# A ConvGLU down projection in Strassen products, alternating with the gate and up products

## The chip, the cores and the metric

One Trainium2 chip, and one of its cores. The metric is the time of one execution on the device in microseconds. Three runs of the kernel before took 2771.68, 2771.95 and 2773.0 us; the median is 2771.95.

## The reference

One layer of a decoder trunk over 512 tokens of width 2048, all in float32: a mixer (a linear recurrence and an RWKV group side by side), then a feed-forward block with a convolution in its gate, then a gated embedding and a last norm. The change concerns the middle one:

```python
        h = h + jnp.concatenate([out_a, out_b], axis=-1) @ w_o[i]

        u = rmsnorm(h, ln_ffn[i])
        gate = causal_dwconv(u @ w_gate[i], conv_f_w[i], conv_f_b[i])
        h = h + (jax.nn.gelu(gate) * (u @ w_up[i])) @ w_down[i]

        u = rmsnorm(h, ln_ple[i])
        e = jax.nn.sigmoid(u @ w_ple_gate[i]) * (p[i] @ w_ple_proj[i])
        h = h + rmsnorm(e, ln_ple_post[i])
```

The hidden width D_FF is 6144, so `w_gate` and `w_up` are 2048 x 6144 and `w_down` is 6144 x 2048. The convolution has three taps and runs along the tokens.

## The kernel before

**Numbers.** To keep float32 accuracy, every operand of a large product is split in two: hi is the operand rounded to the matmul's short format, lo is what is left. A product is three matmuls into the same PSUM bank, whi·xh, whi·xl and wlo·xh (L148, L150, L152 in `dense`).

**The weight queue.** All weights come through one queue. `wfill_` (L103) takes the next item, has SP load it into one of two `wraw` buffers, lets ACT round it to `whi` (L118) and DVE subtract to `wlo` (L119). There are three buffers of each (HL), and the queue runs two items ahead (LOOK): a unit's hi and lo may be written as soon as the unit three before it has been read by PE. Each item is 512 KB, 128 partitions by 1024 numbers. `wnext` hands an item to the matmuls. The Tile scheduler orders each engine's instructions by dependences and priorities; the queue has a raised priority (offw). Nothing is written by hand in the FFN.

**The stages.** `phase1` is the mixer (0 to about 880 us). `phase2` starts with the second half of the output projection w_o, which ends at 955.5 us, and writes the residual `hT`: 16 tiles of 128 features by 512 tokens, features on the partitions. Each of its tiles is scaled by ln_ffn and split into `uh`, `ul` (the list u2). Then comes the FFN:

- `gate_up(f)` makes tile f of 48 of the hidden activation: two groups of 48 matmuls, in which weights stand and the 512 tokens of uh and ul move, 512 columns each. Then DVE scales the gate (L1120) and adds the two earlier taps (L1124), ACT does the first tap and the GELU, POOL multiplies by the norm's factor (L1126), DVE multiplies by up (L1130), and the tile is split: into `xh`, `xl` for chunks 0, 2 and 4, into `hh`, `hl` for chunks 1, 3 and 5. 
- `down(ch)` follows for each chunk of eight tiles (FC = 8, six chunks): 16 output tiles of 24 matmuls each, the chunk's tiles moving, weights standing, and an addition of each into hT on DVE (L1146).
- In the last chunk each finished tile of hT is also scaled and split (u3), squared on ACT and summed on POOL into `acc` (L1159), and transposed by PE, four 128 x 128 blocks (L1162), into `h3`, the residual with tokens on the partitions.

The work of `ffn_order` is plain: eight gate/up tiles, the first tile of the next chunk, then the down product of the finished chunk, and so on.

Behind the FFN, the embedding stage first needs the norm's factor: `tok_rstd` multiplies `acc` by ones on PE (L177) and takes the root on POOL. Then `gate` (L1198 to L1200) multiplies with tokens on the output partitions: blocks of u3 stand and the weights move, 512 columns each. The last stretch of this stage and the output follow; the change gives other buffers to some of its small tiles, since hh and hl are gone.

PSUM has six banks `mm` and two banks `wk`.

Of the kernel before, what the change touches and what calls it, by code (L numbers as in the profile page):

```python
# [21 lines left out]
FC = 8  # L22
# [57 lines left out]
class Builder:  # L80
# [22 lines left out]
    def wfill_(self):  # L103
        nc = self.nc
        while self.wn < len(self.wq) and len(self.wt) < self.LOOK:
            src, shape, *own = self.wq[self.wn]
            self.wn += 1
            if self.wraw:
                raw = self.wraw.pop(0)
            else:  # L110
                raw = self.t(self.cp, "wraw", shape, bufs=self.RAW)
                nc.sync.dma_start(raw, src)
            if own:
                hi, lo = (self.t(self.k2, n, shape, F32R, bufs=1) for n in own)
# [936 lines left out]

    def ffn_order(self):
        nch = NF // FC
        o = []
        for ch in range(nch):
            o += [("f", f) for f in range(ch * FC + (1 if ch else 0), (ch + 1) * FC)]
            if ch + 1 < nch:
                o.append(("f", (ch + 1) * FC))
            o.append(("d", ch))
        return o  # L1060

    def ffn_items(self):
# [3 lines left out]
        for o in self.ffn_order():  # L1066
            if o[0] == "f":
                r += [(A["wgu"][o[1], g, i], u) for g in range(2) for i in range(2)]
            else:
                r += [(A["wd"][o[1], m], u) for m in range(KT)]  # L1070
# [5 lines left out]
        r += [(A["wpg3"][1, 0, :, 2 * i:2 * i + 2], (128, 2, 256), "hl%d" % i, "hl%d" % (2 + i)) for i in range(2)]  # L1076
# [5 lines left out]
    def phase2(self):  # L1082
# [5 lines left out]
        hx = lambda i: (T("hh%d" % i, dt=F32R), T("hl%d" % i, dt=F32R))  # L1088
# [21 lines left out]
        hid = {}  # L1110

        def gate_up(f):
            pg = self.mm()
            self.run(self.dense(pg, 2, u2))
            if f == 0:
                r_ = self.tok_rstd(acc, D, RMS_EPS, k2)
                pu = self.mm()
                self.run(self.dense(pu, 2, u2))
                self.rstd_bcast(acc, D, RMS_EPS, k2, rs, r_)
            V.tensor_tensor(gz[:, 2:S + 2], pg, rs, ALU.mult)  # L1120
            c = T("tmp", 2)
            SC.activation(c, gz[:, 2:S + 2], AF.Identity, scale=self.P("cfw", 2 * NF + f), bias=self.P("cfb", f))
            for w in range(2):
                V.scalar_tensor_tensor(c, gz[:, w:w + S], self.P("cfw", w * NF + f), c, ALU.mult, ALU.add)  # L1124
            SC.activation(c, c, AF.Gelu_apprx_tanh)  # L1125
            G.tensor_tensor(c, c, rs, ALU.mult)  # L1126
            if f:
                pu = self.mm()
                self.run(self.dense(pu, 2, u2))
            V.tensor_tensor(c, c, pu, ALU.mult)  # L1130
            i = f % KT
            hi, lo = self.xsplit(i) if i < 8 else hx(i - 8)
            self.split(hi, lo, c)
            hid[f] = (hi, lo)

        self.acc3 = None
        u3 = []
        h3 = None

        def down(ch):  # L1140
            nonlocal h3
            last = ch == NF // FC - 1
            for m in range(KT):
                pd = self.mm()
                self.run(self.dense(pd, 1, [hid[ch * FC + i] for i in range(FC)]))
                V.tensor_tensor(hT[m], hT[m], pd, ALU.add)  # L1146
                if last:
                    hi, lo = T("uh%d" % m, dt=F32R), T("ul%d" % m, dt=F32R)
                    self.split(hi, lo, hT[m], self.P("ln_ple", m))
                    u3.append((hi, lo))  # L1150
                    if m == 0:
                        self.acc3 = T("acc")
                        SC.activation(self.acc3, hT[m], AF.Square)
                        h3 = [self.bp.tile([128, S], F32, tag="x%s%d" % ("hl"[i // 8], i % 8), name="h3_%d" % i, bufs=1)
                              for i in range(16)]
                    else:
                        sq = T("tmp", 2)
                        SC.activation(sq, hT[m], AF.Square)
                        G.tensor_tensor(self.acc3, self.acc3, sq, ALU.add)  # L1159
                    pt = self.aux()  # L1160
                    for tt in range(4):
                        TE.transpose(pt[:, tt * 128:(tt + 1) * 128], hT[m][:, tt * 128:(tt + 1) * 128], self.K("ident"))  # L1162
                    for tt in range(4):
                        SC.activation(h3[tt * 4 + m // 4][:, (m % 4) * 128:(m % 4 + 1) * 128],
                                      pt[:, tt * 128:(tt + 1) * 128], AF.Copy)

        for o in self.ffn_order():
            gate_up(o[1]) if o[0] == "f" else down(o[1])


        B = lambda i, nm_: T("h%s%d" % ("hl"[i // 8], i % 8))
        BR = lambda i, nm_: T("h%s%d" % ("hl"[i // 8], i % 8), dt=F32R)
        rsp = self.tok_rstd(self.acc3, D, RMS_EPS, k2)
        rsh = k2.tile([128, 4], F32, name="rsh")
# [180 lines left out]
```

## Time and profile before

| what | value |
|---|---|
| median of three runs | 2771.95 us |
| profiled execution | 2769.29 us |
| its span, from the first to the last instruction | 2767.5 us |
| mean granted clock of PE | 0.991 |
| PE busy | 98% of the span |
| FFN, first gate product to last down product | 955.5 to 2541.4 us |
| DMA over the span | 94 GB/s |

A row of instructions in the profile names the line, the engine, the operation and the tiles (output<-inputs), then partitions x elements. PE is the matmul engine, PEld its loading of the standing operand, DVE and ACT the vector and scalar engines, POOL the third elementwise engine, SP the queue that issues DMAs. A row of a wait names the engine and line that waits, and behind `<-` the one that released it. A matmul's busy time is modelled (it overlaps with the next one), so a price for one is taken here from starts, or from a stretch without gaps divided by its count.

### The profile page before, as it was taken

Reading aid. Unit: us, or ns where it says so; the run is one execution under the profiler, and the core shown is the slowest. Engines: PE = TensorE matmul, PEld = TensorE weight load, DVE = VectorE, ACT = ScalarE, POOL = GpSimd, SP = SyncE. Lnnn points to the kernel's source line nnn. Section 1 sums busy time; section 2 is a strip of 40 time slices with the busy share of each in tenths; the row PEclk is TensorE's granted clock in tenths of the full one; section 3 lists DMA queues with packets and bytes.
Section 4 is the critical chain, followed back from the end, with each engine's and each line's share of the span. In section 5 each row is a group of like instructions: output and inputs, shape, how many; then the busy total and the mean of one; then the engine's idle time right before and its main releaser. Section 6 shows DMA issues by size and latency. Waiting matters only on the chain.

```text
span 2767.5 us, 43105 instructions
## 1 busy us (share of the span) xinstructions
PE 2706.2 (98%) x18648; PEld 2216.3 (80%) x18648; DVE 1315.0 (48%) x1761; ACT 955.0 (35%) x1408; POOL 291.4 (11%) x232
## 2 busy tenths in 40 slices
PE   8999999999999999999999999999999999999996
PEld 7877777787787888888888888888888888887886
DVE  7784876668654433333333333333333333344235
ACT  6453455446433322212222222222122212234334
POOL 4010101101111300000000000000000000012013
PEclk9999999999999999999999999999999999999998
DMA  5221221222332322232222222222222222223322
GB/s 170 89 80 57 79 73 60 80 70 92 100 116 81 106 94 97 99 99 92 99 99 92 99 95 96 99 99 92 99 91 99 99 94 97 99 92 111 99 91 99
DMA packets 81886, 261.34 MB, mean 94 GB/s; under 512 B 9504, under 2 KB 12192, under 8 KB 81696
## 3 DMA queue, kind: packets, MB, share of 16 engines
q1 hardware_dynamic: 81696, 258.58, 28.3%
q8 instruction: 146, 2.39, 0.4%
q14 instruction: 44, 0.36, 0.0%
HBM read 250.42 MB, written 8.13 MB: 93 GB/s over the span
## 4 chain that ended last, share of the span: by engine, by line
PE 90%; DVE 5%; ACT 2%; POOL 1%; issue 1%; DMA 1%; SPq 0%; DVEq 0%; POOLq 0%
PE mm L152 25%; PE mm L148 25%; PE mm L150 25%; PE mm L1199 2%; PE mm L1198 2%; PE mm L1200 2%; PE wk L765 2%; PE wk L723 1%; DVE wlo L119 1%; PE wk L732 1%; DVE lrc L595 1%; PE ch L844 0%; PE ch L859 0%; PE wk L902 0%; DVE e L1231 0%
## 5 line engine op out<-in xcount | busy, mean ns | idle before, releaser
L118 ACT ACTIVATE whi<-wraw 128x1024 fp32r<-128x1024 f32 (+2 forms) x449 | 468.4, 1043 | 1368.5 <-PE mm L150 1244.7
L119 DVE TENSOR_TENSOR wlo<-wraw,whi 128x1024 fp32r<-128x1024 f32 (+2 forms) x449 | 554.7, 1235 | 487.0 <-ACT whi L118 482.1
L148 PE MATMUL mm<-uh,whi 128*128 128x512 f32 x1536 | 597.7, 389 | 0.0
L152 PE MATMUL mm<-uh,wlo 128*128 128x512 f32 x1536 | 597.5, 389 | 0.0
L150 PE MATMUL mm<-ul,whi 128*128 128x512 f32 x1536 | 597.5, 389 | 0.0
L148 PE MATMUL mm<-xh,whi 128*128 128x512 f32 x1216 | 481.8, 396 | 1.5 <-DVE y L885 0.9
L152 PE MATMUL mm<-xh,wlo 128*128 128x512 f32 x1216 | 481.3, 396 | 1.5 <-DVE wlo L119 1.5
L150 PE MATMUL mm<-xl,whi 128*128 128x512 f32 x1216 | 480.9, 395 | 0.0
L150 PEld LDWEIGHTS mm<-ul,whi 128*128 128x128 f32 x1536 | 288.3, 188 | 60.0
L152 PEld LDWEIGHTS mm<-uh,wlo 128*128 128x128 f32 x1536 | 288.3, 188 | 59.8
L148 PEld LDWEIGHTS mm<-uh,whi 128*128 128x128 f32 x1536 | 288.3, 188 | 59.8
L152 PEld LDWEIGHTS mm<-xh,wlo 128*128 128x128 f32 x1216 | 229.4, 189 | 52.1 <-issue 2.8
L148 PEld LDWEIGHTS mm<-xh,whi 128*128 128x128 f32 x1216 | 229.7, 189 | 51.6 <-issue 3.8
L150 PEld LDWEIGHTS mm<-xl,whi 128*128 128x128 f32 x1216 | 229.4, 189 | 48.5 <-issue 1.3
L1146 DVE TENSOR_TENSOR hT<-hT,mm 128x512 f32<-128x512 f32 x96 | 66.1, 688 | 320.1 <-PE mm L152 320.1
L1126 POOL TENSOR_TENSOR tmp<-tmp,rsa 128x512 f32<-128x512 f32 x48 | 62.4, 1300 | 1405.1 <-ACT tmp L1125 1405.1
L150 PE MATMUL mm<-hl,whi 128*128 128x512 f32 x384 | 152.9, 398 | 0.0
L148 PE MATMUL mm<-hh,whi 128*128 128x512 f32 x384 | 151.6, 395 | 0.0
L152 PE MATMUL mm<-hh,wlo 128*128 128x512 f32 x384 | 151.6, 395 | 0.0
L1130 DVE TENSOR_TENSOR tmp<-tmp,mm 128x512 f32<-128x512 f32 x48 | 33.0, 688 | 160.5 <-PE mm L152 158.4
L1199 PE MATMUL mm<-wlo,uh 128*128 128x512 f32 (+1 forms) x304 | 107.1, 352 | 0.0
L1200 PE MATMUL mm<-whi,ul 128*128 128x512 f32 (+1 forms) x304 | 107.0, 352 | 0.0
(435 smaller groups left out, 2855.1 us busy)
## 6 DMA issues: line engine op xcount, KB each, us to landing
wraw<-wgu SPq DMA_DIRECT2D x192, 512.0 KB, 3.2
wraw<-wd SPq DMA_DIRECT2D x96, 512.0 KB, 3.2
wraw<-wz SPq DMA_DIRECT2D x80, 512.0 KB, 3.5
wraw<-wpg SPq DMA_DIRECT2D x31, 512.0 KB, 3.3
wraw<-wo SPq DMA_DIRECT2D x24, 512.0 KB, 3.3
wraw<-wo SPq DMA_DIRECT2D x16, 256.0 KB, 2.7
tmp<-xT SPq DMA_DIRECT2D x16, 256.0 KB, 2.7
out<-e SPq DMA_DIRECT2D x16, 256.0 KB, 2.5
```

Of the source, the lines that this page charges most:

```text
L118: nc.scalar.activation(hi, raw, AF.Copy)
L119: nc.vector.tensor_tensor(lo, raw, hi.bitcast(F32), ALU.subtract)
L148: nc.tensor.matmul(ps, hi[:, k, :], xh, start=first and i == 0, stop=False)
L150: nc.tensor.matmul(ps, hi[:, k, :], xl, start=False, stop=False)
L152: nc.tensor.matmul(ps, lo[:, k, :], xh, start=False, stop=last and i == n - 1)
L765: TE.matmul(ps[r_, i * 16:(i + 1) * 16], lhs(r_, c_, i), rhs(r_, i), start=True, stop=True)
L1126: G.tensor_tensor(c, c, rs, ALU.mult)
L1130: V.tensor_tensor(c, c, pu, ALU.mult)
L1146: V.tensor_tensor(hT[m], hT[m], pd, ALU.add)
L1198: TE.matmul(pg[tt], u3[k + i][0][:, ts_], wh[:, i, :], start=k + i == 0, stop=False)
L1199: TE.matmul(pg[tt], u3[k + i][0][:, ts_], wl[:, i, :], start=False, stop=False)
L1200: TE.matmul(pg[tt], u3[k + i][1][:, ts_], wh[:, i, :], start=False, stop=k + i == KT - 1)
```

## The change

The down projection is done another way and at other times.

**Chunks of four tiles.** FC goes from 8 to 4: twelve chunks, 512 hidden features each.

**Seven products.** Of eleven chunks the product is cut into quarters: two halves of the tokens by two halves of the 512 hidden features, and two halves of the weights' rows by two halves of their columns. A Strassen scheme (Winograd's form) makes the four output quarters from seven products of quarters where eight would be plain. It is done for two column halves b, so a chunk has 14 products. `product` has the tokens on the output partitions: 128-token blocks of the activations stand, 512 columns of weights move, 12 matmuls in two PSUM banks for one product. `down` adds each bank to what it belongs to (the table ADDS): directly to h3, the residual with tokens on partitions, or to two running sums `qx` and `qz`, 36 additions a chunk on DVE (line 1267 of the changed kernel). After the last of these chunks 20 additions bring qx and qz into h3.

**Their operands.** `hidden` forms from the four tiles (kept in `raw`) the seven sums of quarters and splits each into hi and lo; the tiles `hid` lie where xh8 to xl15 lay. `down_unit` loads a column half's four weight quarters in turn into `hw0` to `hw3`, and forms the weight sums in place or in `hw4` on DVE (lines 1091, 1094, 1100, 1104); every product's weight then goes through the queue as an item of the same size as before, split on lines 121 and 122. The weight array `wd` is laid out anew on the host.

**The order.** `ffn_order` alternates: after the chunk's four tiles and the first of the next, a product, then a half of a gate or up tile (24 matmuls) of the next chunk, and so on; 12 such halves are spread over the 14 products. Gate and up of all tiles from the fifth on use the two `wk` banks.

**The last chunk** is done plainly (`down_last`), 512 columns by 512 columns: two units of 24 matmuls each, then four additions to h3.

**Transposes.** h3 is now needed from the start: `turn` transposes hT in 64 blocks during the first four tiles. And the embedding stage needs features on partitions: `to_features` transposes h3 back after each column block of the last chunk, 64 blocks, and splits them out of PSUM into u3 (hi on ACT, lo on DVE).

**The norm's factor.** `to_features` squares on ACT with a running sum per token (`ss3`), and DVE and POOL turn these into the factor beside the embedding stage's first products. POOL's sum `acc` and the step through PE are gone there.

The diff, cut to its core:

```diff
-FC = 8
+FC = 4
...
-            if self.wraw:
+            if callable(src):
+                raw = src()
+            elif self.wraw:
                 raw = self.wraw.pop(0)
...
     def ffn_order(self):
+        g = lambda f: [("g", f, w, h) for w in range(2) for h in range(2)]
+        o = sum([g(f) for f in range(FC)], [])
         nch = NF // FC
-        o = []
-        for ch in range(nch):
-            o += [("f", f) for f in range(ch * FC + (1 if ch else 0), (ch + 1) * FC)]
-            if ch + 1 < nch:
-                o.append(("f", (ch + 1) * FC))
-            o.append(("d", ch))
+        for ch in range(nch - 1):
+            q = [("q", ch, b, i) for b in range(2) for i in range(7)]
+            o += g((ch + 1) * FC)
+            n = sum([g((ch + 1) * FC + i) for i in range(1, FC)], [])
+            k = 0
+            for i, x in enumerate(q):
+                o.append(x)
+                e = (i + 1) * len(n) // len(q)
+                o += n[k:e]
+                k = e
+        o += [("d", cb, kh) for cb in range(4) for kh in range(2)]
         return o
+    def down_unit(self, ch, b, i):
...
+        if i == 0:
+            self.q = {(0, 0): load(0, 0), (0, 1): load(0, 1)}
+            return self.q[0, 0]
+        if i == 1:
+            self.q[1, 1] = load(1, 1)
+            self.qt = self.t(self.k2, "hw4", (128, 2, 512), bufs=1)
+            V.tensor_tensor(self.qt, self.q[0, 0], self.q[0, 1], ALU.add)
+            return self.qt
+        if i == 2:
+            V.tensor_tensor(self.qt, self.qt, self.q[1, 1], ALU.add)
+            return self.qt
+        if i == 3:
+            self.q[1, 0] = load(1, 0)
+            return self.q[1, 1]
+        if i == 4:
+            V.tensor_tensor(self.q[0, 1], self.q[0, 1], self.q[1, 1], ALU.add)
+            return self.q[0, 1]
+        if i == 5:
+            return self.q[1, 0]
+        V.tensor_tensor(self.qt, self.qt, self.q[1, 0], ALU.add)
+        return self.qt
...
-        hx = lambda i: (T("hh%d" % i, dt=F32R), T("hl%d" % i, dt=F32R))
...
+        def turn(cb):
+            for tt in range(4):
+                pt = self.mm()
+                for i in range(4):
+                    TE.transpose(pt[:, i * 128:(i + 1) * 128], hT[4 * cb + i][:, tt * 128:(tt + 1) * 128], self.K("ident"))
+                SC.activation(h3[tt * 4 + cb], pt, AF.Copy)
...
+            d = tile(F32)
+            o = [None] * 7
+            o[0] = pair(a(0, 0))
+            V.tensor_tensor(d, a(1, 0), a(1, 1), ALU.subtract)
+            o[1] = pair(d)
+            V.tensor_tensor(d, d, a(0, 0), ALU.subtract)
+            o[2] = pair(d)
+            V.tensor_tensor(d, d, a(0, 1), ALU.add)
+            o[3] = pair(d)
+            V.tensor_tensor(d, a(0, 0), a(1, 0), ALU.subtract)
+            o[4] = pair(d)
+            o[5] = pair(a(0, 1))
+            o[6] = pair(a(1, 1))
+            return o
...
+        ADDS = [[(QX, ALU.add), (st(0, 0), ALU.add)], [(QZ, ALU.add)], [(QX, ALU.add)], [(st(0, 1), ALU.add)],
+                [(st(1, 1), ALU.subtract), (st(1, 0), ALU.add)], [(st(0, 0), ALU.add)], [(st(1, 0), ALU.add)]]
+
+        def product(ps, x, w, tt, first, last):
+            ts_ = slice(tt * 128, (tt + 1) * 128)
+            for k in range(2):
+                TE.matmul(ps, x[0][:, k, ts_], w[0][:, k, :], start=first and k == 0, stop=False)
+                TE.matmul(ps, x[0][:, k, ts_], w[1][:, k, :], start=False, stop=False)
+                TE.matmul(ps, x[1][:, k, ts_], w[0][:, k, :], start=False, stop=last and k == 1)
+
+        def down(ch, b, i):
+            w = self.wnext()
+            ps = [self.mm(), self.mm()]
+            for tt in range(2):
+                product(ps[tt], self.hids[ch][i], w, tt, True, True)
+            for at, op in ADDS[i]:
+                for tt in range(2):
+                    o = at(tt, b)
...
+                        V.tensor_tensor(o, o, ps[tt], op)
+
+        def down_last(cb, kh):
+            if kh == 0:
+                self.pd = [self.mm() for tt in range(4)]
+            w = self.wnext()
+            for tt in range(4):
+                product(self.pd[tt], self.hids[NF // FC - 1][kh][tt // 2], w, tt % 2, kh == 0, kh == 1)
+            if kh == 1:
+                for tt in range(4):
+                    h = h3[tt * 4 + cb]
+                    V.tensor_tensor(h, h, self.pd[tt], ALU.add)
...
+        def to_features(cb):
+            for tt in range(4):
+                sq = T("tmp", 2)
+                SC.activation(sq, h3[tt * 4 + cb], AF.Square, accum_out=ss3[:, tt * 4 + cb:tt * 4 + cb + 1])
+            for m in range(4 * cb, 4 * cb + 4):
+                pt = self.aux()
+                for tt in range(4):
+                    TE.transpose(pt[:, tt * 128:(tt + 1) * 128], h3[tt * 4 + cb][:, (m % 4) * 128:(m % 4 + 1) * 128], self.K("ident"))
+                hi, lo = T("uh%d" % m, dt=F32R), T("ul%d" % m, dt=F32R)
+                self.split(hi, lo, pt, self.P("ln_ple", m))
+                u3[m] = (hi, lo)
...
-        rsp = self.tok_rstd(self.acc3, D, RMS_EPS, k2)
...
+                V.tensor_reduce(t_.unsqueeze(2), ss3.rearrange("p (t c) -> p t c", c=4), mybir.AxisListType.X, ALU.add)
...
-    o["wd"] = f(g["w_down"][0].reshape(NF // FC, FC, 128, KT, 128).transpose(0, 3, 2, 1, 4))
+    o["wd"] = f(g["w_down"][0].reshape(NF // FC, 2, 2, 128, 2, 2, 512).transpose(0, 5, 1, 4, 3, 2, 6))
```

Two places show how the instructions stand in the rows. The first is PE near the end of the down projection, in the kernel before: the last chunk's first tile of the residual (hT1 here) is transposed inside the matmuls of the next output tile (mm is a PSUM bank, wk the transposed tile, con the identity):

```order
L152 MATMUL mm_2694_19739<-hh0_2493_18174,wlo_2681_19632 128x512
L148 MATMUL mm_2694_19739<-hh1_2574_18820,whi_2680_19631 128x512
L1162 MATMUL wk_2693_19730<-con_59,hT1_8388 128x128 x4
L150 MATMUL mm_2694_19739<-hl1_2575_18821,whi_2680_19631 128x512
L152 MATMUL mm_2694_19739<-hh1_2574_18820,wlo_2681_19632 128x512
```

In the changed kernel, PE at the end of the first of the last chunk's four column blocks. The block's tiles h3_0, h3_4, h3_8 and h3_12 hold the four token blocks:

```order
L1254 MATMUL mm_3206_20871<-whi_3193_20823,hid_3202_20865 128x512
L1291 MATMUL wk_3217_20944<-con_59,h3_0_10621 128x128
L1291 MATMUL wk_3217_20944<-con_59,h3_4_10625 128x128
L1291 MATMUL wk_3217_20944<-con_59,h3_8_10629 128x128
L1291 MATMUL wk_3220_20953<-con_59,h3_0_10621 128x128
L1291 MATMUL wk_3220_20953<-con_59,h3_4_10625 128x128
L1291 MATMUL wk_3220_20953<-con_59,h3_8_10629 128x128
L1252 MATMUL mm_3229_20980<-whi_3208_20874,hid_3195_20852 128x512
L1291 MATMUL wk_3217_20944<-con_59,h3_12_10633 128x128
L1291 MATMUL wk_3220_20953<-con_59,h3_12_10633 128x128
```

The transposes have moved from the middle of the next tile's matmuls to right behind the unit whose sums they read; one matmul of the next block stands between them.

The second place is DVE. In the kernel before, in the down product of the first chunk, it has these rows (wlo is a weight's lo part, hT the residual):

```order
L119 TENSOR_TENSOR wlo_1742_12198<-wraw_1740_12195,whi_1741_12197 128x1024
L1146 TENSOR_TENSOR hT11_8398<-hT11_8398,mm_1739_12194 128x512
L119 TENSOR_TENSOR wlo_1746_12230<-wraw_1744_12227,whi_1745_12229 128x1024
L1146 TENSOR_TENSOR hT12_8399<-hT12_8399,mm_1743_12226 128x512
L119 TENSOR_TENSOR wlo_1750_12262<-wraw_1748_12259,whi_1749_12261 128x1024
```

In the changed kernel, DVE at the start of a column half of a later chunk, where two products follow each other (hw4 and hw2 hold weight sums and quarters, qx and h3 what the products are added to, row and tmp belong to the gate of the next chunk's tile):

```order
L1192 TENSOR_TENSOR row_1537_10619<-wk_2983_19523,rsa_87 128x512
L122 TENSOR_TENSOR wlo_3000_19620<-wraw_2998_19617,whi_2999_19619 128x1024
L1196 SCALAR_TENSOR_TENSOR tmp_2997_19611<-row_1537_10619,par_58,tmp_2997_19611 128x512
L1267 TENSOR_TENSOR qx_1538_10637<-qx_1538_10637,mm_3001_19623 128x512
L1196 SCALAR_TENSOR_TENSOR tmp_2997_19611<-row_1537_10619,par_58,tmp_2997_19611 128x512
L1267 TENSOR_TENSOR qx_1538_10637<-qx_1538_10637,mm_3002_19624 128x512
L122 TENSOR_TENSOR wlo_3004_19643<-hw4_2994_19580,whi_3003_19642 128x1024
L1267 TENSOR_TENSOR h3_1_10622<-h3_1_10622,mm_3001_19623 128x512
L1104 TENSOR_TENSOR hw4_2994_19580<-hw4_2994_19580,hw2_3011_19693 128x1024
L122 TENSOR_TENSOR wlo_3010_19666<-wraw_3008_19663,whi_3009_19665 128x1024
```

Where one addition stood between two splits, there now stand additions out of two banks, a weight sum and the gate's convolution.

More of the change, by code (lines that the diff above doesn't have):

```diff
@@ L113, in wfill_ @@
             if own:
-                hi, lo = (self.t(self.k2, n, shape, F32R, bufs=1) for n in own)
+                w = self.t(self.k2, own[0], (128, 2) + shape[1:], F32R, bufs=1)
+                hi, lo = w[:, 0], w[:, 1]
             else:
@@ L1108, in phase2 @@
         G.memset(gz[:, 0:2], 0.0)
[L1110 to L1155, printed above, removed]
-                    else:
[L1157 to L1165, printed above, removed]
@@ L1167, in phase2 @@
[L1167 to L1177 removed]
+        h3 = [self.bp.tile([128, S], F32, tag="x%s%d" % ("hl"[i // 8], i % 8), name="h3_%d" % i, bufs=1) for i in range(16)]
@@ new lines, in turn, with half @@
+        def turn(cb):
[4 more added lines that the diff above has]
+                SC.activation(h3[tt * 4 + cb], pt, AF.Copy)
+        def half(ps, us, h):
+            wh, wl = self.wnext()
+            for k in range(8):
+                xh, xl = us[8 * h + k]
+                TE.matmul(ps, wh[:, k, :], xh, start=h + k == 0, stop=False)
+                TE.matmul(ps, wh[:, k, :], xl, start=False, stop=False)
+                TE.matmul(ps, wl[:, k, :], xh, start=False, stop=h == 1 and k == 7)
@@ new lines, in phase2, with gate_up @@
+        raw = [None, None]
+        pgu = [None, None]
+        gc = None
+        def gate_up(f, which, h):
+            nonlocal gc
+            if h == 0:
+                pgu[which] = self.aux() if f >= FC else self.mm()
+            half(pgu[which], u2, h)
+            if h == 0:
+                return
+            if which == 0:
+                if f == 0:
+                    self.r2 = self.tok_rstd(acc, D, RMS_EPS, k2)
+                    return
+            elif f == 0:
+                self.rstd_bcast(acc, D, RMS_EPS, k2, rs, self.r2)
+            if which == 0 or f == 0:
+                V.tensor_tensor(gz[:, 2:S + 2], pgu[0], rs, ALU.mult)
+                gc = c = T("tmp", 2)
+                SC.activation(c, gz[:, 2:S + 2], AF.Identity, scale=self.P("cfw", 2 * NF + f), bias=self.P("cfb", f))
+                for w in range(2):
+                    V.scalar_tensor_tensor(c, gz[:, w:w + S], self.P("cfw", w * NF + f), c, ALU.mult, ALU.add)
+                SC.activation(c, c, AF.Gelu_apprx_tanh)
+                G.tensor_tensor(c, c, rs, ALU.mult)
+            if which == 1:
+                i = f % FC
+                if i % 2 == 0:
+                    raw[i // 2] = T("hw%d" % (5 + i // 2), 1, (128, 2, 512))
+                V.tensor_tensor(raw[i // 2][:, i % 2, :], gc, pgu[1], ALU.mult)
+                if i < 4:
+                    turn(i) if f < FC else None
+                if i == FC - 1:
+                    self.hids[f // FC] = hidden(f == NF - 1)
@@ new lines, in phase2, with hidden, tile, pair @@
+        a = lambda i, j: raw[j][:, :, 256 * i:256 * i + 256]
+        def hidden(last):
+            n = 0
+            def tile(dt):
+                nonlocal n
+                t = self.bp.tile([128, 2, 256], dt, tag="x%s%d" % ("hl"[n // 8], 8 + n % 8), name=self.nm("hid"), bufs=1)
+                n += 1
+                return t
+            def pair(src):
+                hi, lo = tile(F32R), tile(F32R)
+                self.split(hi, lo, src)
+                return hi, lo
+            if last:
+                return [[pair(a(i, j)) for i in range(2)] for j in range(2)]
+            d = tile(F32)
[12 more added lines that the diff above has]
+            return o
@@ new lines, in phase2 @@
+        for o in self.ffn_order():
+            if o[0] == "g":
+                gate_up(*o[1:])
+            elif o[0] == "q":
+                down(*o[1:])
+                if o[1:] == (NF // FC - 2, 1, 6):
+                    for b in range(2):
+                        for q, at, op in ((QX, st(1, 0), ALU.add), (QX, st(0, 1), ALU.subtract), (QZ, st(0, 1), ALU.add),
+                                          (QX, st(1, 1), ALU.subtract), (QZ, st(1, 1), ALU.add)):
+                            for tt in range(2):
+                                V.tensor_tensor(at(tt, b), at(tt, b), q(tt, b), op)
+            else:
+                down_last(*o[1:])
+                if o[2] == 1:
+                    to_features(o[1])
```

70 lines of the change are left out of this document (47 added, 23 removed).

## The prediction

> **What bounds the kernel now.** I read the page's engine shares first, then the list of what PE waits for, then the stretches of the FFN one by one.
>
> ```profile
> span 2767.5 us, 43105 instructions
> PE 2706.2 (98%) x18648; PEld 2216.3 (80%) x18648; DVE 1315.0 (48%) x1761; ACT 955.0 (35%) x1408; POOL 291.4 (11%) x232
> ...
> PE 90%; DVE 5%; ACT 2%; POOL 1%; issue 1%; DMA 1%; SPq 0%; DVEq 0%; POOLq 0%
> ```
>
> ```profile
> PE wk L177 <- POOL acc L1159: 1.1, 1, 1.1
> ```
>
> PE is busy for 98% of the span and carries 90% of the chain that ended last. The row below the page's is the whole list of PE's waits from 955 to 2600 us: one wait, at the step out of the FFN. Inside the FFN there is none, so it costs what its matmuls cost. The next view cuts it into stretches (from and to, length, then busy time of PE, PEld, DVE, ACT, POOL with instruction counts, granted clock, DMA share, GB/s). The first two rows are the start and the first eight gate/up tiles, the next five are down chunks 0 to 4, then chunk 5 with its transposes, then the step into the embedding stage. The last row is a piece of the output projection before the FFN.
>
> ```profile
> 955.53:979.05 23.52, 23.52 (x113) 19.71 (x112) 6.38 (x7) 6.18 (x7) 3.77 (x2) 1.00 0.26 90
> 979.05:1153.25 174.20, 174.20 (x771) 144.24 (x770) 68.40 (x75) 50.31 (x59) 11.70 (x9) 1.00 0.29 97
> 1153.25:1240.29 87.04, 87.04 (x385) 72.07 (x384) 31.22 (x33) 17.54 (x18) 0.00 (x0) 1.00 0.29 97
> 1414.37:1503.96 89.59, 89.59 (x385) 72.08 (x384) 31.27 (x33) 17.56 (x18) 0.00 (x0) 1.00 0.28 94
> 1678.06:1765.10 87.04, 87.04 (x386) 72.07 (x384) 31.21 (x33) 17.54 (x18) 0.00 (x0) 1.00 0.29 97
> 1939.18:2028.77 89.59, 89.59 (x386) 72.07 (x384) 31.25 (x33) 17.57 (x18) 0.00 (x0) 1.00 0.28 94
> 2202.86:2289.90 87.04, 87.04 (x385) 72.07 (x384) 31.21 (x33) 17.54 (x18) 0.00 (x0) 1.00 0.29 97
> 2442.22:2541.35 99.13, 99.13 (x454) 77.99 (x452) 45.01 (x51) 46.43 (x110) 24.03 (x14) 1.00 0.29 94
> 2541.35:2549.47 8.12, 6.99 (x29) 5.42 (x28) 1.92 (x4) 1.47 (x6) 2.78 (x2) 0.79 0.81 245
> 890.50:901.40 10.90, 10.90 (x50) 9.03 (x49) 10.10 (x13) 8.57 (x15) 5.32 (x4) 1.00 0.52 168
> ```
>
> A chunk has 384 matmuls, so one costs 87.04/384 = 0.2267 us, with no gap at all. Chunks 1 and 3 take 89.59 (0.2333 each); their moving tiles are hh and hl, where chunks 0, 2 and 4 stream xh and xl. DVE has 31 us of work in 87, so it is far from the limit today.
>
> **The change, part by part.**
>
> *Matmuls removed.* The first eleven chunks of four tiles now cost 14 products of 12 matmuls, 11 x 168 = 1,848, and the twelfth stays plain with 192: 2,040 instead of 2,304. Each still moves 512 columns, but weights move and activations stand. The gate stage of the embedding does that already:
>
> ```profile
> 2600.08 0.39 PE L1199 MATMUL mm<-wlo,uh 128*128 128x512 f32 x1
> ...
> 2603.94 0.39 PE L1198 MATMUL mm<-whi,uh 128*128 128x512 f32 x1
> ```
>
> The second starts 17 matmuls after the first: 3.86/17 = 0.227, the same price. The tiles hh and hl are gone; the products read whi, wlo and tiles in the old xh8 to xl15 slots. I take 0.2267 for all 2,040, 462.5 us; the upper bound is 0.2333, the price with hh and hl, which adds 13.6.
>
> What they replace: chunks 0 to 4, 3 x 87.04 + 2 x 89.59 = 440.3; chunk 5, 99.13 less four early embedding matmuls (0.9), 98.2, its transposes included. And the step into the embedding stage:
>
> ```profile
> 2542.59 0.40 PE L1251 MATMUL mm<-whi,hl 128*128 128x512 f32 x1
> 2544.11 1.05 PE L177 MATMUL wk<-con,acc 128*128 128x1 f32 x8 [1.13 <-POOL acc L1159]
> ...
> 2546.32 0.63 PE L1200 MATMUL mm<-whi,ul 128*128 128x512 f32 x1
> ...
> 2548.88 0.52 PE L1200 MATMUL mm<-whi,ul 128*128 128x512 f32 x1
> ```
>
> PE waits 1.13 us for POOL's running sum of squares, does eight one-column products, and then runs six matmuls in 2.56 us, 0.427 each, at a clock that the window row gives as 0.79 on average. In 8.12 us start 18 full matmuls, worth 4.1; the other 4.0 us are wait, small products and half clock. The change takes that sum with accumulating squares on ACT and DVE and has no PE step there, so the 4.0 go. Before: 440.3 + 98.2 + 4.0 = 542.5 us.
>
> *What a gap costs.* The Trainium skill's page "TensorE: Matmul & The Clock Gate" (Part 1, What's actually happening) says that the clock halves only after a whole idle window of about 3.4 us. The trace differs: here 1.13 us idle and a thin spell of small products were enough, and the slow matmuls behind them, some eight at 0.2 us extra, cost another 1.6 us. By the page a 1 us wait would cost 1 us, by the row up to 2.8, and my upper bounds use the row.
>
> *Transposes added.* Chunk 5 now has 64; the change has 64 early (turn, four batches of 16 after the first four tiles) and 64 late (to_features).
>
> ```profile
> 2448.76 0.66 PE L1162 MATMUL wk<-con,hT 128*128 128x128 f32 x4
> ...
> 2454.85 0.66 PE L1162 MATMUL wk<-con,hT 128*128 128x128 f32 x4
> ```
>
> Between these lie 24 matmuls of 0.2333 (5.60) in 6.09 us: 0.5 us for four. 32 such fours: 16 us. Bounds: by columns, a quarter of 0.2267 each, 7.3; by the rows' own busy time, 0.66 for four, 21.
>
> *Late waits.* After each late pair of down units PE transposes what DVE has just added (the first pair of order pieces in the section on the change). Before, one unit's matmuls stood between a transpose and its addition; now only six short transposes and one matmul do, and two wk tiles then have to be split before the next two. The cover is about 0.8 us against one addition of 0.688 (row below) and its semaphores. I take 1 us a block, 4 us; bounds 0 and 4 x 2.8 = 11.
>
> *DVE and ACT.* This is where the change could give its gain back. DVE rows of the FFN (by form; mean ns of one is the number before the second bar):
>
> ```profile
> L119 DVE TENSOR_TENSOR wlo<-wraw,whi 128x1024 fp32r<-128x1024 f32 x272 | 333.3, 1225 | 344.5 <-ACT whi L118 340.3 <-PE wk L190 4.2
> L1124 DVE SCALAR_TENSOR_TENSOR tmp<-row,par,tmp 128x512 f32<-128x512 f32 x96 | 71.9, 749 | 2.6 <-ACT tmp L1122 0.9
> L1146 DVE TENSOR_TENSOR hT<-hT,mm 128x512 f32<-128x512 f32 x80 | 55.1, 688 | 269.3 <-PE mm L152 269.3
> L1120 DVE TENSOR_TENSOR row<-mm,rsa 128x512 f32<-128x512 f32 x48 | 33.2, 692 | 154.2 <-PE mm L152 154.2
> L132 DVE TENSOR_TENSOR xl<-tmp,xh 128x512 fp32r<-128x512 f32 x24 | 16.5, 686 | 0.0
> ```
>
> ```profile
> L118 ACT ACTIVATE whi<-wraw 128x1024 fp32r<-128x1024 f32 x272 | 288.6, 1061 | 1006.0 <-PE mm L150 1001.4 <-PE mm L152 4.7
> ```
>
> A new chunk of four tiles has on DVE: 30 weight splits (16 gate/up, 14 products) and 8 weight sums of the same shape, 38 x 1.225 = 46.6; 36 additions out of PSUM, 24.8; four tiles of convolution and product, 4 x (0.692 + 2 x 0.749 + 0.688) = 11.5; seven splits and four forms of the activations, 11 x 0.686 = 7.5. That is 90 us beside PE's 552 x 0.2267 = 125: DVE goes from some 38% to 72%, and ACT does 30 x 1.061 and a few more, below 45. Both fit. Order matters more. Before, in a down chunk, DVE alternates one split and one addition for each 24 matmuls, 5.44 us (the second pair of order pieces). At the densest place now, the start of a column half with two products in a row, splits stand behind additions that wait for PE. But a split may start when the unit three before it is done, that is 5.44 us (two products) or 8.16 us (a product and a half tile) before PE needs it, and takes 1.06 + 1.225 = 2.3. DVE's additions in between, at most four of 0.688 and one sum, are 4.0 us in the tightest case, so a little is left. I cost this at nothing. The 890.50 row above is the nearest: there PE ran 12 matmuls a weight unit and bank, 2.72 us each, with DVE busy 10.10 of 10.90 us, and never waited. That stretch also receives two or three weight sums, which the order moves ahead into it; its splits were 2 to 3 us early, so 1 us, bounds 0 and 2.5.
>
> *Sum.* After: 462.5 + 16 + 4 = 482.5, against 542.5; with the 1 us ahead a gain of 59. The profiled execution took 2769.3 us (span 2767.5); the median of three runs, 2771.95, lies 2.7 above. Forecast 2771.95 - 59 = 2713. With all low ends 2699, with all high ends 2740; they will hardly all meet, so its own range is 2702 to 2735.
>
> **The rivals.**
>
> *DVE is late at the joins.* If at each of the 22 starts of a column half a split comes one split late, PE waits 22 x 1.225 = 27: 2740. If each wait also halves the clock, 22 x 2.8 = 62, and the gain is gone: 2775. For it: 90 us of DVE come in bursts. Against it: the 890.50 row.
>
> *DVE sets the pace (slower).* Every product waits for its weights, because splits queue behind PSUM additions of the product before. 154 products x 1.225 = 189: 2902. It decides from 59/154 = 0.38 us a product on. For it: a strict queue, with three kinds of waits in it; against it: the 5.44 us of lead and 28% of free DVE.
>
> *Bank cycling.* PE keeps changing banks in groups of six, micro-idles between them, and its clock falls: 1,848 matmuls at 0.427 add 370, about 3083. The same skill page (A second HAM failure mode: psum-queue depth-cycling) describes such a loss at 512 columns. Against it: the 890.50 row, 12 a bank at clock 1.00.
>
> **How the numbers follow.** Forecast 0.78; late at the joins 0.11 (0.08 without the clock, 0.03 with it); DVE sets the pace 0.08; bank cycling 0.03. The range takes the forecast's own and most of the 0.08: 2700 to 2744. A measurement can tell 0.2% from no change, 5.5 us: faster 0.78 + 0.08 = 0.86, the same 0.03, slower 0.11.
>
> **What would show it.** Right: PE at 98% in the FFN; products at 0.227 a matmul; a chunk in about 125 us, against 174.1 for eight gate/up tiles; DVE near 72% there; PE waiting only in the last 45 us of the FFN, under 2 us a block. Wrong: PE waits on wlo (L122) in the list of waits, a granted clock below 1.00 in the chunks, or products at 0.233.

## The result, and the profile after

The changed kernel takes 2708.63 us (median of four runs, 2707.82 to 2710.31) against 2771.81 for the kernel before, whose runs now number four. The ratio is 0.977, with a 95% interval of 0.9756 to 0.9785: 63 us faster. The forecast was 59 us less, 2713. The page after, engine shares and chain:

```profile
span 2706.0 us, 43401 instructions
PE 2646.9 (98%) x18440; PEld 2175.3 (80%) x18440; DVE 1735.8 (64%) x2321; ACT 1051.0 (39%) x1483; POOL 291.1 (11%) x217
...
PE 90%; DVE 5%; ACT 2%; POOL 1%; issue 1%; DMA 1%; SPq 0%; DVEq 0%; POOLq 0%
```

PE is what it was, 98% busy, with 208 instructions fewer. DVE has 421 us more to do, and PE doesn't notice: the list of PE's waits has no row at all between 945 and 2600 us. The windows of the changed kernel (from and to, length, busy time of PE, PEld, DVE, ACT, POOL, clock, DMA share, GB/s) show the first four gate and up tiles, two whole periods of a chunk, the first column block of the last chunk, and two later ones with their transposes:

```profile
959.45:1077.19 117.74, 117.74 (x562) 98.73 (x560) 47.66 (x54) 41.36 (x56) 10.25 (x7) 1.00 0.26 85
1207.75:1332.87 125.12, 125.12 (x554) 103.60 (x552) 85.81 (x103) 41.46 (x45) 7.67 (x4) 1.00 0.30 101
2208.71:2333.83 125.12, 125.12 (x554) 103.60 (x552) 85.52 (x102) 41.45 (x45) 7.70 (x4) 1.00 0.31 101
2431.75:2442.63 10.88, 10.88 (x49) 8.96 (x48) 6.23 (x8) 4.92 (x9) 0.00 (x0) 1.00 0.30 96
2442.63:2455.55 12.92, 12.92 (x66) 10.52 (x65) 7.82 (x10) 7.20 (x15) 0.00 (x0) 1.00 0.25 82
2468.45:2481.36 12.91, 12.91 (x65) 10.51 (x64) 7.82 (x10) 7.20 (x15) 0.00 (x0) 1.00 0.25 83
```

A period is 552 matmuls in 125.12 us, 0.2267 each, to the last digit the price of before, with weights moving and with the matmuls of two kinds of work alternating. DVE is at 85.8/125.12 = 69%.

To compare kernels without the mixer ahead of the FFN, one stretch is used from here on: from the first gate product of the FFN to the hundredth product of the embedding's gate. Timeline rows of PE, kernel before:

```profile
955.53 0.39 PE L148 MATMUL mm<-uh,whi 128*128 128x512 f32 x1
...
2572.49 0.39 PE L1198 MATMUL mm<-whi,uh 128*128 128x512 f32 x1
```

And the changed one:

```profile
959.45 0.39 PE L1170 MATMUL mm<-uh,whi 128*128 128x512 f32 x1
...
2511.32 0.39 PE L1339 MATMUL mm<-whi,uh 128*128 128x512 f32 x1
```

1616.96 us before, 1551.87 after: 65.1 us less. The FFN's start 3.9 us later is not the change's: kernels below that share the mixer's code with the kernel before start it at 958.9 and 960.8. The same stretch of each experiment, read the same way, with the medians (each ratio is taken against runs of the kernel before that were made beside that experiment, with medians from 2771.04 to 2773.20):

| kernel | stretch, us | median, us | ratio to the kernel before, 95% interval |
|---|---|---|---|
| before | 1616.96 | 2771.81 | |
| changed | 1551.87 | 2708.63 | 0.9756 to 0.9785 |
| e1_no_alternation | 1600.12 | 2758.62 | 0.9938 to 0.9973 |
| e2_plain_eight | 1611.69 | 2765.67 | 0.9968 to 0.9987 |
| e3_dve_2 | 1559.46 | 2713.80 | 0.9779 to 0.9812 |
| e3_dve_4 | 1565.13 | 2720.99 | 0.9798 to 0.9831 |
| e9_reads_2 | 1551.89 | 2704.98 | 0.9737 to 0.9766 |
| e9_reads_4 | 1566.92 | 2721.82 | 0.9794 to 0.9827 |
| e10_no_priority | 1551.93 | 2708.66 | 0.9750 to 0.9782 |
| e7_after_moved_128 | 1583.46 | 2741.48 | 0.9880 to 0.9909 |
| e6_moved_128 | 1610.27 | 2764.91 | 0.9963 to 0.9983 |
| e8_no_step | 1614.63 | 2770.79 | 0.9988 to 1.0006 |

### The profile page after: what moved, and what is told of

Its sections match the earlier page's. It is cut to its first block, busy times and chain, and to the rows that moved or that the text cites. A ratio compares the mean times of both kernels' runs of the same rounds, so it can differ in the third digit from the quotient of the medians.

```text
span 2706.0 us, 43401 instructions
## 1 busy us (share of the span) xinstructions
PE 2646.9 (98%) x18440; PEld 2175.3 (80%) x18440; DVE 1735.8 (64%) x2321; ACT 1051.0 (39%) x1483; POOL 291.1 (11%) x217
## 4 chain that ended last, share of the span: by engine, by line
PE 90%; DVE 5%; ACT 2%; POOL 1%; issue 1%; DMA 1%; SPq 0%; DVEq 0%; POOLq 0%
PE wk L1171 12%; PE wk L1170 12%; PE wk L1172 12%; PE mm L155 7%; PE mm L153 7%; PE mm L151 7%; PE mm L1253 6%; PE mm L1252 6%; PE mm L1254 6%; PE mm L1341 2%; PE mm L1339 2%; PE mm L1340 2%; PE wk L768 2%; PE mm L1170 1%; PE mm L1172 1%; PE mm L1171 1%
## 5 line engine op out<-in xcount | busy, mean ns | idle before, releaser
L1170 PE MATMUL wk<-uh,whi 128*128 128x512 f32 x1408 | 547.8, 389 | 0.0
L1171 PE MATMUL wk<-ul,whi 128*128 128x512 f32 x1408 | 547.7, 389 | 0.0
L1172 PE MATMUL wk<-uh,wlo 128*128 128x512 f32 x1408 | 547.7, 389 | 0.0
L1172 PEld LDWEIGHTS wk<-uh,wlo 128*128 128x128 f32 x1408 | 264.3, 188 | 54.9
L1170 PEld LDWEIGHTS wk<-uh,whi 128*128 128x128 f32 x1408 | 264.3, 188 | 54.9
L1171 PEld LDWEIGHTS wk<-ul,whi 128*128 128x128 f32 x1408 | 264.3, 188 | 54.8
L122 DVE TENSOR_TENSOR wlo<-hw,whi 128x1024 fp32r<-128x1024 f32 x154 | 188.7, 1225 | 181.0 <-ACT whi L121 178.5
L1253 PE MATMUL mm<-wlo,hid 128*128 128x512 f32 x680 | 265.1, 390 | 0.0
L1254 PE MATMUL mm<-whi,hid 128*128 128x512 f32 x680 | 264.8, 389 | 0.0
L1252 PE MATMUL mm<-whi,hid 128*128 128x512 f32 x680 | 264.8, 389 | 0.0
L1267 DVE TENSOR_TENSOR h<-h,mm 128x512 f32<-128x512 f32 x264 | 175.2, 682 | 0.6
```

The lines of the kernel that those rows point to most:

```text
L122: nc.vector.tensor_tensor(lo, raw, hi.bitcast(F32), ALU.subtract)
L1170: TE.matmul(ps, wh[:, k, :], xh, start=h + k == 0, stop=False)
L1171: TE.matmul(ps, wh[:, k, :], xl, start=False, stop=False)
L1172: TE.matmul(ps, wl[:, k, :], xh, start=False, stop=h == 1 and k == 7)
L1252: TE.matmul(ps, x[0][:, k, ts_], w[0][:, k, :], start=first and k == 0, stop=False)
L1253: TE.matmul(ps, x[0][:, k, ts_], w[1][:, k, :], start=False, stop=False)
```

## The experiments

The theory behind the forecast: the FFN lasts as long as its matmuls, DVE's new work fits beside them, and small parts of the gain come from the tiles hh and hl and from the step into the embedding stage. The rivals: DVE late at the joins, DVE setting the pace, or a gain that has another source than the number of matmuls.

### Eight products instead of seven

Every chunk is done plainly, as the last one is, in the new layout and alternating with the gate and up halves.

```diff
-            q = [("q", ch, b, i) for b in range(2) for i in range(7)]
+            q = [("d", cb, kh, ch) for cb in range(4) for kh in range(2)]
...
-                    self.hids[f // FC] = hidden(f == NF - 1)
+                    self.hids[f // FC] = hidden(True)
```

> Every chunk is done as the last one is: eight units of 24 matmuls, alternating with the gate and up halves, same layout, same transposes, no weight sums, no qx and qz. My theory (PE's matmul count sets the time): 264 matmuls more of 0.2267, +59.8: 2768, no wait of PE in the FFN, and only about 4 us better than the kernel before. Rival (the gain comes from the rest: the alternation, the tiles, the step into the embedding stage): 2709 to 2730.

The stretch is 59.8 us longer than the changed kernel's, 264 x 0.2267 = 59.8, again with no wait of PE. So the count of matmuls is worth what it says, and everything else in the change together (alternation, other tiles, transposes, the step) is worth 1616.96 - 1611.69 = 5.3 us.

### No alternation

```diff
             for i, x in enumerate(q):
                 o.append(x)
-                e = (i + 1) * len(n) // len(q)
-                o += n[k:e]
-                k = e
+            o += n
```

> The fourteen products of a chunk run one after the other, with no gate or up halves between them; nothing else changes. My theory (the alternation is what hides DVE): behind the trace, a chunk's products bring DVE 14 splits of 1.225, 8 sums of 1.225 and 36 additions of 0.68, about 52 us, and PE needs 38.1 for them. DVE can be behind by some three products (six banks), 4 to 6 us a chunk, so PE loses 8 to 14 us in each of 11 chunks: 2795 to 2860, with waits of PE on wlo. Rival (DVE is busy for 68% of the FFN, which is enough wherever its work stands): 2709, as the changed kernel.

It costs 48.3 us of the 65: the alternation is what makes room for DVE. But it costs less than was expected, and by another wait. PE's list of waits in this kernel:

```profile
PE mm L1250 <- DVE h L1265: 34.4, 30, 2.8
```

PE never waits for a weight (wlo). It waits for a bank that DVE has not added up yet, three times in most chunks (2.76, 0.15 and 0.45 us in the chunk shown next). Windows of the same kernel, the fourteen products of a chunk and then the rest of its period:

```profile
1333.68:1375.01 41.33, 37.84 (x163) 30.12 (x162) 40.21 (x49) 14.87 (x14) 0.00 (x0) 1.00 0.28 91
1375.01:1463.42 88.41, 88.41 (x392) 73.28 (x391) 44.70 (x53) 26.51 (x31) 5.20 (x4) 1.00 0.30 101
```

DVE is busy 40.2 of 41.3 us there. The 52 us expected were priced by the durations of the records. In a dense queue the records overlap, as DVE's timeline of that stretch shows:

```profile
1355.51 1.23 DVE L122 TENSOR_TENSOR wlo<-hw,whi 128x1024 fp32r<-128x1024 f32 x1
1356.65 0.68 DVE L1265 TENSOR_TENSOR h<-h,mm 128x512 f32<-128x512 f32 x1
1357.24 1.22 DVE L1102 TENSOR_TENSOR hw<-hw,hw 128x1024 f32<-128x1024 f32 x1
1358.38 1.88 DVE L1265 TENSOR_TENSOR h<-h,mm 128x512 f32<-128x512 f32 x3
1360.24 1.23 DVE L122 TENSOR_TENSOR wlo<-hw,whi 128x1024 fp32r<-128x1024 f32 x1
```

From start to start a split takes 1.14 us where its record says 1.23, an addition 0.59 to 0.62 where it says 0.68. So by an estimate from these starts the products need 46.7 us of DVE, (14 + 8) x 1.14 + 36 x 0.6, and about 5 of them run on into the next stretch. What DVE is late by shows as PE's three waits, 3.4 us together; with the slower restarts behind them the period is 4.6 us longer (129.74 against 125.12).

### More work for DVE

First operations that wait for nothing, two or four for each product, ahead of its additions:

```diff
             w = self.wnext()
+            for _ in range(2):
+                V.tensor_tensor(acc, acc, acc, ALU.max)
```

> Two operations of 128 x 512 on DVE are added ahead of each of the 154 products' additions; their result is not used. DVE goes from 85.5 to about 104.8 us in a chunk's 125.1. My theory (a split is done 3.1 us or more ahead of PE, and at the tightest place, two products in a row, 4 x 0.69 = 2.75 us come in): no change, 2706 to 2713. Rival (DVE's queue is strict and what stands in it ahead of a split is paid at the joins): 22 x 2.75 = 60: 2769.

> Four such operations for each product: DVE about 124.0 of 125.1 us in a chunk, so by its sum it still fits. My theory (the lead decides, 3.1 us at the tightest place, and 8 x 0.69 = 5.5 come in there): PE waits 2.4 us at 22 places, 53 us, and up to 35 more where the clock halves behind it: 2762 to 2797, waits on wlo at the second half tile after two products. Rival (only the pace decides): 2709 to 2715.

Neither theory met it. The stretch grows by 7.6 and by 13.3 us, far less than 60, but not by nothing. PE's waits, first with two:

```profile
PE wk L1172 <- DVE wlo L122: 4.8, 4, 2.1
PE mm L1253 <- DVE wlo L122: 1.2, 1, 1.2
```

and with four:

```profile
PE wk L1172 <- DVE wlo L122: 9.0, 9, 2.2
PE mm L1253 <- DVE wlo L122: 1.2, 1, 1.2
```

With two they fall in the first four chunks only, with four in the first nine. An operation that depends on nothing is put wherever the scheduler finds it ready, so the extra work is not spread over the eleven chunks as was expected: it fills DVE in the first ones, ahead of some splits, until it is used up. Two periods of the kernel with two operations, the second chunk's and a later one:

```profile
1209.87:1335.96 126.09, 124.83 (x551) 103.07 (x550) 124.86 (x164) 40.88 (x45) 6.15 (x4) 1.00 0.31 100
1588.50:1713.62 125.12, 125.12 (x554) 103.65 (x553) 85.51 (x102) 41.45 (x45) 7.70 (x4) 1.00 0.31 101
```

DVE is at 99% in the first and as in the changed kernel in the second. So these two kernels show what a full DVE costs, some 1 us a period here, and say little about the load of 105 of 125 us that was to be tested, or about the places in question. The next pair puts work where the change has its own, behind the matmuls:

```diff
                         V.tensor_tensor(o, o, ps[tt], op)
+            for tt in range(2):
+                for _ in range(1):
+                    V.tensor_tensor(acc, acc, ps[tt], ALU.max)
```

> The changed kernel, with one more DVE operation of 128 x 512 on each of the two banks of a product, behind the additions; its result is not used. Unlike the free operations of the two runs before, these wait for PE and stand in DVE's queue between splits. Priced by the starts of a dense queue, 0.61 us, a chunk's DVE work goes from 85.5 to about 102.6 of 125.1 us. Theory (the lead decides; the smallest is 3.1 us, behind two products in a row): 2 x 2 x 0.61 = 2.4 us come in there, which is less: FFN as long as before, 2706 to 2713. Rival (what queues ahead of a split is paid at once): 22 x 2.4 = 53: 2762.

> Two such operations on each bank: DVE about 119.7 of 125.1 us in a chunk. Theory (the lead decides): 4.9 us come in where 3.1 are left, so PE waits 1.8 us at 22 places, 40 us, and some 0.4 more for each restart: 2750 to 2760, the waits on wlo in the half tile behind two products. Rival (the sum of DVE's work decides, and it still fits): 2709 to 2715.

With two the stretch is 1551.89 us, the same to 0.02 (its profiled execution is 2.3 us shorter, and its FFN started 2.3 us earlier, at 957.1). With four, the window of a period and the list of PE's waits:

```profile
1207.62:1332.74 125.12, 125.12 (x553) 103.60 (x552) 117.77 (x159) 41.24 (x45) 6.25 (x4) 1.00 0.30 101
```

```profile
PE mm L1254 <- DVE hid L135: 7.8, 1, 7.8
PE mm L1252 <- DVE acc L1270: 3.9, 2, 2.3
```

DVE is at 94% and the period is still 125.12. The only three waits stand in the last chunk, where the 20 corrections and the additions queue up behind the load. They are 11.7 us together, PE's clock is at 0.50 for 13.65 us from 2438.0 on, and the stretch is 15 us longer. So neither theory was right on the four: the 22 waits did not come, and by the load alone there should have been none. In the steady part of the FFN DVE has some 32 us of room in a period for work that stands behind the matmuls; at 99%, with work ahead of splits, it has none.

### The split's place in DVE's queue

Why was the lead not eaten up? The next idea was the queue's raised priority, which lets splits go ahead of additions. Without it in the second phase:

```diff
-        with self.tc.high_priority(offset=W['offw']):
+        with self.tc.high_priority(offset=self.OFFW):
...
         self.MM = 6
+        self.OFFW = 0
```

> The changed kernel without the raised priority of the weight queue in the second phase, so that DVE's splits stand where the program has them, behind the additions of the product before. Theory (what the forecast cost at nothing is free because a split goes ahead of the additions that wait for PE): behind two products in a row the next half tile's split now stands behind the additions of the second product, so PE waits for two additions and a split, 2 x 0.6 + 1.2 less the two matmuls that need only whi, some 2 us, at 22 places: 44 us and more with the restarts: 2750 to 2770, waits on wlo. Rival (the lead comes from the three buffers alone, the place in DVE's queue doesn't matter at 68%): 2709.

That theory fell: 1551.93 and no wait in the FFN, though the order did change. (One wait on a split, 0.62 us, stands ahead of the FFN, in the second half of w_o.) What explains it is the changed kernel's own timeline at such a join. Two products run from 1577.67, and the next half tile starts at 1583.11. DVE:

```profile
1578.79 1.23 DVE L122 TENSOR_TENSOR wlo<-wraw,whi 128x1024 fp32r<-128x1024 f32 x1 [0.16 <-ACT whi L121]
1579.93 0.68 DVE L1267 TENSOR_TENSOR qx<-qx,mm 128x512 f32<-128x512 f32 x1
1580.52 0.68 DVE L1267 TENSOR_TENSOR h<-h,mm 128x512 f32<-128x512 f32 x1
1581.12 0.68 DVE L1267 TENSOR_TENSOR qx<-qx,mm 128x512 f32<-128x512 f32 x1
1581.73 1.23 DVE L122 TENSOR_TENSOR wlo<-hw,whi 128x1024 fp32r<-128x1024 f32 x1
```

The split for 1583.11 is the first of them. It could start when the half tile before the two products ended, at 1577.67; ACT and DVE need 2.35 us to 1580.02, and 5.44 - 2.35 = 3.09 us of lead are left. Nothing stands in between, because the first product's first bank is full only after its six matmuls, at about 1579.0; its additions come behind the split. The split that does stand behind additions, at 1581.73, belongs to the product at 1588.55 and ends 5.6 us ahead. It stands behind three of the two products' four additions; without the priority it stands behind all four, and the first split where it was. Aligning all splits with their units gives a smallest lead of 3.09 us in the changed kernel, 3.04 with two reads, 2.81 with four, and 3.09 without the priority. That DVE's order at the joins is harmless with or without the priority at this load is shown. Without the priority it was not tried with a fuller DVE; with it, 94% cost nothing in the steady part when the work stood behind the matmuls, and 99%, with work ahead of splits, cost some 1 us a period.

### Where the moving tiles lie

Chunks 1, 3 and 5 of the kernel before, whose moving tiles are hh and hl, pay 0.2333 us a matmul. The theory is that hh and hl begin at multiples of 256 bytes of a partition and all other moving tiles 128 bytes off one. The traces hold no addresses, so what is tested is a shift by 128 bytes. In the kernel before, 128 unused bytes ahead of them:

```diff
         hid = {}
+        pad = k2.tile([128, 32], F32, name="pad")
+        V.memset(pad, 0.0)
```

> The kernel before, with 128 unused bytes ahead of the tiles hh and hl, so that these begin 128 bytes further on; all other tiles stay. Theory (the 0.2333 us of a matmul in chunks 1, 3 and 5 comes from where the moving tiles lie: hh and hl begin at multiples of 256 bytes, all other moving tiles 128 bytes off one): those 1,152 matmuls go to 0.2267, -7.6: 2764. Rival (it comes from something else in those chunks): no change, 2772, chunk 1 again at 89.6.

And in the changed kernel the same two lines ahead of all tiles of the second phase, which by the theory puts uh and ul on multiples of 256:

> The changed kernel, with 128 unused bytes ahead of all tiles of the second phase, so that uh and ul, which move in the gate and up products, begin at multiples of 256 bytes. Theory (the place of a moving tile sets its rate): 4,608 matmuls go from 0.2267 to 0.2333, +30.6: 2739, eight half tiles at 5.6 instead of 5.44. Rival (the rate does not come from the place): 2709.

Both came as the theory of the place says. Chunk 1 in the kernel with hh and hl moved, first and 128th of its matmuls with hh and whi (of 128):

```profile
1417.76 0.39 PE L148 MATMUL mm<-hh,whi 128*128 128x512 f32 x1
...
1504.12 0.39 PE L148 MATMUL mm<-hh,whi 128*128 128x512 f32 x1
```

381 matmuls in 86.36 us, 0.2267, where the kernel before takes 0.2333; the stretch shrinks by 6.7 us, 2.55 in each of chunks 1 and 3 and the rest, 1.6, mainly in chunk 5, which transposes interrupt. With uh and ul moved it grows by 31.6 (4,608 matmuls x 0.0066 = 30.4). A part of the remaining 1.2 us shows that it is not the moving operand alone. In the embedding's gate uh and ul stand and the weights move, and the weights' buffers were not shifted. Its first column block, 192 matmuls, in the changed kernel with uh and ul moved:

```profile
2517.12 0.39 PE L1341 MATMUL mm<-whi,uh 128*128 128x512 f32 x1
...
2561.50 0.39 PE L1343 MATMUL mm<-whi,ul 128*128 128x512 f32 x1
```

From the first to the last of them are 44.38 us, 0.2324 each; in the changed kernel itself the same 192 matmuls run from 2488.86 to 2532.17, 0.2268 each.

### The step into the embedding stage

The kernel before, with its factor taken from four columns of the running sum on DVE (the sum over the partitions is left out):

```diff
-        rsp = self.tok_rstd(self.acc3, D, RMS_EPS, k2)
+        rsp = k2.tile([128, 4], F32, name="rsp0")
+        V.tensor_scalar(rsp, self.acc3[:, 0:4], 1.0 / D, RMS_EPS, ALU.mult, ALU.add)
```

> The kernel before without its step through PE into the embedding stage: the factor is made from four columns of the running sum on DVE instead of the eight one-column products (which leaves out the sum over the partitions). Theory (wait, small products and half clock cost 4.0 us there): 2768, and the granted clock of that window near 1.00. Rival (the next products are late for another reason): 2772.

The median can't tell it from no change. The stretch says 2.3 us, not 4.0. Timeline of PE behind the FFN in this kernel:

```profile
2553.26 0.39 PE L1201 MATMUL mm<-whi,ul 128*128 128x512 f32 x1
2554.78 0.50 PE L1252 MATMUL mm<-whi,hl 128*128 128x512 f32 x1 [1.13 <-ACT hl L131]
2555.11 0.39 PE L1253 MATMUL mm<-wlo,hl 128*128 128x512 f32 x1
2555.34 0.40 PE L1252 MATMUL mm<-whi,hl 128*128 128x512 f32 x1
```

The slow matmuls and the eight small products are gone. A wait of 1.13 us has come back a little later, on another operand of the embedding: a wait took the place of the one removed. In the changed kernel PE has no wait at either place. That the whole 4.0 counts there is not shown by this run; it rests on the sum in the next section.

## Why the prediction was right

- **The matmuls.** Forecast 462.5 us at 0.2267. Measured: a product of 12 takes 2.72, a plain column block of 48 takes 10.88, 154 x 2.72 + 4 x 10.88 = 462.4. The upper bound of 0.2333 was excluded by the tiles' places, as e6_moved_128 and e7_after_moved_128 show.
- **Before.** Of the 65.1 us, the count is worth 59.8 (e2_plain_eight). The other 5.3 are the faster rate of the 1,152 matmuls that had moved hh and hl (7.7 by the two rates, 6.7 in e6_moved_128) and the step (4.0 by the rows of before, of which e8_no_step shows 2.3), less the added transposes: 14.9 us (next point), where chunk 5 of the kernel before had 98.2 - 384 x 0.2333 = 8.6. 7.7 + 4.0 - 6.3 = 5.4.
- **Transposes and late waits.** Forecast 16 + 4 for all of them. The early ones in the changed kernel:

```profile
983.05 1.91 PE L1163 MATMUL mm<-con,hT 128*128 128x128 f32 x16
984.72 0.48 PE L1170 MATMUL mm<-uh,whi 128*128 128x512 f32 x1
```

Sixteen take 1.67 us, 0.42 for four where 0.5 was assumed: 6.7 in all. A late block is 12.92 where its matmuls need 10.88: four times 2.0 is 8.2. That is 14.9 against 20, the largest error of the sum, and 4 of these 5.1 us are the 1 us a block of waits that was assumed: there is none on PE's list. For the stretch alone the forecast is 542.5 - 482.5 = 60; with these 5.1 it is the 65.1 us by which the stretch is shorter. The rows of such a block:

```profile
2442.63 0.82 PE L1291 MATMUL wk<-con,h 128*128 128x128 f32 x6
2443.21 0.48 PE L1252 MATMUL mm<-whi,hid 128*128 128x512 f32 x1
2443.58 0.44 PE L1291 MATMUL wk<-con,h 128*128 128x128 f32 x2
...
2445.95 0.33 PE L1291 MATMUL wk<-con,h 128*128 128x128 f32 x1
```

The six and two transposes with one matmul between them follow without a gap: the "cover of 0.8 us" was enough.
- **DVE.** Costed at nothing, and it costs nothing, but the reason given does not hold. In its tightest case the prediction has 5.44 us from a split's release to its use, 2.3 for rounding and split, and up to 4.0 of additions and a sum in between: that is some 0.8 us too much, and yet "a little is left". So the zero did not follow from its own numbers, and in that it was lucky. The rows show nothing in between at the tightest place and 3.1 us left, because the products' banks fill later than the split is ready. The forecast of 72% was 69%.
- **The microsecond ahead of the FFN** is not seen: from the first matmul of the second phase to the FFN PE has no further wait, and that takes 72.9 us (886.55 to 959.45) against 72.7 before (882.83 to 955.53).
- **The rivals.** DVE late at the joins, DVE setting the pace and bank cycling all need a wait or a clock below 1.00 in the chunks; there is neither. That "every product waits because splits queue behind PSUM additions" is refuted in its mechanism: no split was late in the FFN's steady part, neither with DVE at 94% (e9_reads_4) nor, at the load of the change, without the priority (e10_no_priority). In the FFN late splits appear only in e3_dve_2 and e3_dve_4, with DVE at 99%, and cost some 1 us a chunk there, not 14 splits of 1.225.

## What to carry to other kernels

Where PE is the bound and never waits, the value of fewer matmuls is their count times the measured period, provided the added elementwise work is spread beside other matmuls: here the same products without the alternation gave back 48 of 65 us. To see whether a strict queue will be late, follow one operand: when its buffer comes free, what can be ready to stand ahead of it, when it is needed; counting the instructions between two rows of an order says less. And price a busy queue by starts, not by the durations of its records.

## What the runs showed of the hardware

**An operand's place.** A 512-column matmul took 0.2333 us or 0.2267, and a shift of its moving tile by 128 bytes in the partition turned one into the other. This is shown in both directions, on 384 matmuls a chunk (hh, hl) and on 4,608 (uh, ul). With uh and ul as standing operands the move cost nearly the same, 0.2324 against 0.2268. That the slow places are multiples of 256 bytes is the theory, as no trace holds an address; why they are slow is not shown, nor whether other offsets have other prices.

**The clock after a gap.** The kernel without alternation has ten waits of 2.76 or 2.77 us, all at the same place of a chunk. Windows of 3 us behind the first three:

```profile
1225.06:1228.06 3.00, 3.00 (x7) 2.42 (x8) 3.00 (x4) 0.00 (x0) 0.00 (x0) 0.50 0.00 0
1355.64:1358.64 3.00, 2.87 (x11) 2.07 (x12) 3.00 (x4) 0.00 (x0) 0.00 (x0) 1.00 0.00 0
1485.38:1488.38 3.00, 2.87 (x12) 2.06 (x12) 3.00 (x4) 0.00 (x0) 0.00 (x0) 1.00 0.00 0
```

The clock fell to one half behind the first and stayed at 1.00 behind the other nine. What differs is where the gap lies. Up to the end of the FFN the stretches at half clock in this trace are 3.41 or 6.83 us long, and the one at 1224.90 begins 100 times 3.413 us after the one before it, at 883.56. In steps of that length, the one that holds most of the first gap, and the two that share the second:

```profile
1221.48:1224.90 3.42, 0.81 (x4) 0.35 (x2) 3.42 (x5) 1.06 (x1) 0.00 (x0) 1.00 0.23 92
1351.19:1354.60 3.41, 1.69 (x8) 1.07 (x6) 3.36 (x5) 0.30 (x2) 0.00 (x0) 1.00 0.43 149
1354.60:1358.02 3.42, 2.25 (x9) 1.59 (x10) 3.41 (x5) 0.87 (x1) 0.00 (x0) 1.00 0.00 0
```

PE was busy for 0.81 us of the step ahead of the half clock. The second gap is split between two steps, and the eight later ones lie much as it does. PE's busy time does not order all cases: in the kernel before, 1.13 us and eight small products halved the clock (the step from 2542.32 to 2545.73 is 2.28 us busy, 0.9 of it with these products); in the one without that step 1.13 us alone did not. The Trainium skill's page "TensorE: Matmul & The Clock Gate" (Part 1, What's actually happening) has the clock decided over free-running windows of some 3.4 us. The steps of 3.413 us agree with a free-running window; that a step in which PE was busy for 0.81 us halves the clock does not agree with a whole idle window. So a short wait has no fixed price: here the same 2.8 us of idle time kept the clock nine times and halved it once, and the fourteen products of that chunk took 42.19 us against 41.33 in the next.
